# Issuing the stick-breaking scores of two heads interleaved on two halves of TensorE's rows, in one transformer stack on one Trainium2 core

## The chip, the core and the metric

One core of one Trainium2 chip runs the whole program as one launch. The metric is device time in microseconds (us): the median of several executions. The engines are TensorE (PE), VectorE (DVE), ScalarE (ACT), GpSimd (POOL) and SyncE (SP, which here issues the DMAs).

## What is computed

A block of one layer (dilated and sliding-window attention, gated, then an MLP) is followed by a block of two layers; width 1024, 512 positions, all in fp32. Each layer of the second block is a feed-forward part, a mixer with three branches, and a feed-forward part. The branches are stick-breaking attention (4 heads of 64), a chunkwise mLSTM (4 heads of 128) and MLA, a causal softmax attention (4 heads). The change touches the first of them. For one head, with z the scaled scores of a query against the keys before it:

```python
z = jnp.einsum('bhqd,bhkd->bhqk', qb, k[:, :, :n]) * scale      # scale = 64 ** -0.5
log_keep = jnp.where(mask, jax.nn.log_sigmoid(-z), 0.0)
later = ...                       # sum of log_keep over the keys between key and query
w = jnp.where(mask, jnp.exp(jax.nn.log_sigmoid(z) + later), 0.0)
out = jnp.einsum('bhqk,bhkd->bhqd', w, v[:, :, :n])
```

The kernel takes log_sigmoid from exp(-|z|) and a logarithm, so it needs |z|.

## The kernel before

**Main stream.** Nearly all of the time goes into products with weights. A weight tile is loaded by DMA (`load_w`, L346), rounded by ACT to `whi` (L348), its rest formed by DVE as `wlo` (L349); three products of 128x128 weights with up to 512 columns (`mm3`, `mm3t`) stand for one in fp32. In a layer's mixer the stream is: the latent projection (`c`), q, k and v of the stick-breaking branch, then `ml_proj`, which is eight feature tiles (PSUM tile `pf`, `fm_proj`) and two token projections (`pt`, `tm`) into `mlv` and `mgo`; then a wait for "mlw"; then per branch eight times a gate (`pgate`) and a branch product (`pbr`).

**Planner.** The order of PE is written out by hand, and no other engine's: `Loom` holds jobs (generators) beside the main stream. It has a clock of its own, `now`, which each matmul moves by a cost written in `mm` and `tr` (L175 and L182; 0.2135 for 512 columns of the weight products, twice 0.107 or 8.34e-4 a column for an fp32 product, 0.107 for a transpose). At the end of each half of a feature tile (12 products, 2.56 planner's us) and of each six products in a token projection (1.28), `turn()` runs, in the order of the list, every job whose due time has come and whose condition holds. A job that yields a number is due that much later; one that yields a function waits for it. Where the main stream itself must wait (`loom.wait`), jobs are stepped at once, whatever their due time, and their matmuls stand in PE's order with no weight product between. The jobs of a mixer are, in the order of the list, MLA (`mla_job`, then three workers that share 16 units of scores `mls`, transposes `mlT` and outputs `mlo`), stick-breaking (`sb_job`), and the gates of the mLSTM (`ml_gates_job`), which goes on only when "sb" and "ymla" are ready, makes `mwt` and sets "mlw".

**Slots.** The larger tiles live in a fixed set of places (`Slots`): 18 of 4352 bytes a partition and 5 of 2048. A tile takes the smallest place that fits. `room(...)` is the condition that so many places of these sizes are free. A place taken by the main stream without room steps jobs until there is some. In a mixer the large ones go to q, k, v of this branch (3), MLA's values and transposed heads (5, given back when its last unit is done), `ymla`, four `mlqk`, `ysb`, two `mlv`, two `mgo`, and the tiles of `stick_head`.

**The branch.** A pair of heads lies in the two halves of 128 partitions: head `hf` of pair `pr` has rows 64 hf to 64 hf + 63 of `q[:, pr]` and `k[:, pr]`. `stick_head` (L1365) runs once per head: it takes three score tiles at once, z, t and sp, each a place of 1024 columns (4096 bytes) and one of 256; writes the scores of four key blocks (512, 384, 256 and 128 query columns) into three banks `sbs` (L175) in three groups; ACT copies each bank to z (L1380) and its absolute value to t (L1381); Exp and Ln on t (L1383, L1384), two combinations on DVE into sp and z (L1385, L1386), and POOL masks the diagonals (L1395). After `T_SB` = 9.0 the running sums go out as four products `sbl`, from the last key block to the first; between two of them lies a DVE addition of one row (L1405) and a pause `T_SBR` = 1.5. Then DVE subtracts (L1408), ACT takes Exp (L1411), POOL masks (L1414), and t and sp are given back. When both heads of a pair have their weights, `sb_unit` waits `T_SBW` = 2.0 and issues the product with the values, `sbo`, whose two heads write the two column halves; z of both is given back. `sb_job` runs the four heads one after the other.

Of the kernel before, what the change touches and what calls it, by code (L numbers as in the profile page):

```python
# [12 lines left out]
AF = mybir.ActivationFunctionType  # L13
# [4 lines left out]
S = 512  # L18
# [108 lines left out]
class Net:  # L127
# [920 lines left out]
    def mixer(self, l, g_next):  # L1048
        nc, a, T, H, loom = self.nc, self.a, self.tiny, self.H, self.loom
        self.layer = l  # L1050
        w, b_in = a["w_in_2"][l], a["b_in_2"][l]
        V, A, G = nc.vector, nc.scalar, nc.gpsimd
# [28 lines left out]
        sbt = sq, sk, sv = [self.duo("sbq"), self.duo("sbk"), self.tok("sbv")]  # L1081
# [13 lines left out]

        W = {}

        def sb_unit(pr, hf):
            yield from self.stick_head(sq, sk, pr, hf, W)
            if len(W) < 2:  # L1100
                return
            yield T_SBW
            po = self.bank("sbo")
            for kb in range(TB):
                for hf in range(2):
                    h = 2 * pr + hf
                    self.mm(po[hf * 64:hf * 64 + 64, kb * 128:S], sv[:, kb, h * 64:h * 64 + 64], self.tri(W[hf], kb),
                            kb == 0, kb == TB - 1)
            H.put(*W[0], *W[1])
            W.clear()  # L1110
            if pr == 0:
                yield lambda: H.room(4096)
                ysb.append(self.duo("ysb"))
            A.copy(ysb[0][:, pr], po)
            if pr == 1:
                H.put(*sbt)
                ready.add("sb")

        def sb_job():
            for pr in range(2):  # L1120
                for hf in range(2):
                    yield from sb_unit(pr, hf)
        loom.add(sb_job())


# [236 lines left out]
        return t[1 if kb == 2 else 0][:, o:o + n]  # L1362


    def stick_head(self, q, k, pr, hf, W):  # L1365

        nc, H = self.nc, self.H
        V, A, G = nc.vector, nc.scalar, nc.gpsimd
        groups = ((1, 3), 0, 512, 1024), ((2,), 1, 0, 256), ((0,), 0, 0, 512)
        hs = slice(hf * 64, hf * 64 + 64)  # L1370
        yield lambda: H.room(4096, 4096, 4096, 1024, 1024, 1024)
        z, t, sp = self.tri_tiles("sbz"), self.tri_tiles("sbt"), self.tri_tiles("sbp")
        for kbs, i, c0, c1 in groups:
            ps = self.bank("sbs")
            c = 0
            for kb in kbs:
                n = S - kb * 128
                self.mm(ps[:, c:c + n], k[hs, pr, kb * 128:(kb + 1) * 128], q[hs, pr, kb * 128:S], True, True)
                c += n
            A.activation(z[i][:, c0:c1], ps[:, 0:c], AF.Copy, scale=0.125)  # L1380
            A.activation(t[i][:, c0:c1], ps[:, 0:c], AF.Abs, scale=0.125)  # L1381
        for i in range(2):
            A.activation(t[i], t[i], AF.Exp, scale=-1.0)  # L1383
            A.activation(t[i], t[i], AF.Ln, bias=1.0)  # L1384
            V.scalar_tensor_tensor(sp[i], z[i], 0.0, t[i], op0=ALU.max, op1=ALU.add)  # L1385
            V.scalar_tensor_tensor(z[i], z[i], 0.0, t[i], op0=ALU.min, op1=ALU.subtract)  # L1386

        keep = t[0][0:1, 0:768]
        own = {3: keep[:, 0:128], 2: keep[:, 128:384], 1: keep[:, 384:768]}
        for kb in (3, 2, 1, 0):  # L1390
            if kb:
                A.copy(own[kb], self.tri(sp, kb)[0:1])
                G.memset(own[kb][:, 0:1], 0.0)
            d = self.tri(sp, kb)[:, 0:128]
            G.tensor_mul(d, d, self.upper0)  # L1395
        yield T_SB
        pl = {1: self.bank("sbl"), 2: self.bank("sbl")}
        pl[3] = pl[1][:, 384:512]
        for kb in (3, 2, 1, 0):
            n = S - kb * 128  # L1400
            if kb == 0:
                pl[0] = self.bank("sbl")
            self.mm(pl[kb][:, 0:n], self.trigt, self.tri(sp, kb), True, True)
            if kb:
                V.tensor_add(self.tri(sp, kb - 1)[0:1, 128:n + 128], pl[kb][0:1, 0:n], own[kb])  # L1405
                yield T_SBR
        for i, c0, c1, kb in ((0, 512, 1024, 1), (1, 0, 256, 2), (0, 0, 512, 0)):
            V.tensor_sub(z[i][:, c0:c1], z[i][:, c0:c1], pl[kb][:, 0:c1 - c0])  # L1408
        H.put(*t, *sp)
        for i in range(2):  # L1410
            A.activation(z[i], z[i], AF.Exp)  # L1411
        for kb in range(TB):
            d = self.tri(z, kb)[:, 0:128]
            G.tensor_mul(d, d, self.upper)  # L1414
        W[hf] = z


    def ml_gates_job(self, ifg, W, ready):
# [225 lines left out]
```

## Time and profile before

| | us |
|---|---|
| median of three runs (lowest, highest) | 2348.06 (2347.34, 2348.90) |
| the profiled execution | 2348.01 |
| its span, first to last instruction | 2346.3 |
| PE busy | 2331.9 (99%) |
| DVE, ACT, POOL busy | 1275.5, 905.1, 381.3 |
| chain that ended last, share of PE | 98% |
| of it PE `sbs`, `sbl` | 1% each |

The page gives busy time by engine, then the span in slices, the DMA queues, the chain of work that ended last, and the costliest groups of instructions. A group's busy time is what its instructions cover, so that overlapping ones count once; the mean is of one instruction. An fp32 product shows as two records. All matmuls carry the line of the helper `mm` (L175) or `tr` (L182), so they are told apart by tile.

### The profile page before, as it was taken

The numbers are of one execution on the slowest core, as the hardware profiler recorded it, in microseconds if no ns is written. First come the engines' busy times: TensorE is split into PE (matmuls) and PEld (weight loads), VectorE is DVE, ScalarE is ACT, GpSimd is POOL, SyncE is SP. The second block draws the span as 40 slices with busy tenths as digits, with TensorE's granted clock in tenths as the row PEclk, the third lists the DMA queues.
The fourth block names the chain that finished last, engine by engine and source line by source line (L and its number), as shares of the span: only waits on it lengthen the run. The fifth ranks groups of instructions, "written<-read, shape, count | busy, mean of one in ns | idle before, by whom it ended". The sixth has DMA issues, their size and how long they took to land.

```text
span 2346.3 us, 28790 instructions
## 1 busy us (share of the span) xinstructions
PE 2331.9 (99%) x11064; PEld 1946.7 (83%) x11064; DVE 1275.5 (54%) x2214; ACT 905.1 (39%) x1510; POOL 381.3 (16%) x385
## 2 busy tenths in 40 slices
PE   8999999999999999999999999999999999999999
PEld 7899888888888888877888888888888778888887
DVE  7744556435355545785554554455458755446552
ACT  6645433222223223676333333223236572333321
POOL 2000014101022112211111321211211110113110
PEclk9999999999999999999999999999999999999999
DMA  4212432333323323322233333333232232323332
GB/s 137 64 55 73 121 96 90 101 97 95 103 86 100 101 92 98 87 65 85 72 90 99 99 95 94 94 95 99 90 101 82 72 86 58 105 81 108 91 102 87
DMA packets 250462, 213.71 MB, mean 91 GB/s; under 512 B 14166, under 2 KB 234068, under 8 KB 250324
## 3 DMA queue, kind: packets, MB, share of 16 engines
q1 hardware_dynamic: 250324, 211.87, 30.4%
q8 instruction: 87, 1.43, 0.2%
q14 instruction: 51, 0.42, 0.1%
HBM read 208.64 MB, written 3.19 MB: 90 GB/s over the span
## 4 chain that ended last, share of the span: by engine, by line
PE 98%; DMA 1%; ACT 0%; DVE 0%; SPq 0%; issue 0%; ACTq 0%
PE pd L175 15%; PE pgate L175 15%; PE pt L175 15%; PE pg L175 10%; PE pa L175 10%; PE pu L175 7%; PE pf L175 6%; PE po L175 5%; PE pbr L175 5%; PE mls L175 1%; PE sbs L175 1%; PE mnum L175 1%; PE sbl L175 1%; PE mss L175 1%; PE mlo L175 1%; PE s L175 1%
## 5 line engine op out<-in xcount | busy, mean ns | idle before, releaser
L349 DVE TENSOR_TENSOR wlo<-wraw,whi 128x1024 fp32r<-128x1024 f32 (+3 forms) x394 | 546.5, 1387 | 415.3 <-ACT whi L348 411.3
L348 ACT CAST whi<-wraw 128x1024 fp32r<-128x1024 f32 (+3 forms) x394 | 404.6, 1028 | 666.7 <-PE pg L175 141.9
L175 PE MATMUL pd<-hidh,whi 128*128 128x512 f32 x520 | 202.3, 389 | 0.0
L175 PE MATMUL pd<-hidl,whi 128*128 128x512 f32 x520 | 202.3, 389 | 0.0
L175 PE MATMUL pd<-hidh,wlo 128*128 128x512 f32 x520 | 202.3, 389 | 0.0
L175 PE MATMUL pgate<-xh,whi 128*128 128x512 f32 x512 | 201.2, 393 | 0.0
L175 PE MATMUL pgate<-xh,wlo 128*128 128x512 f32 x512 | 199.4, 390 | 0.0
L175 PE MATMUL pgate<-xl,whi 128*128 128x512 f32 x512 | 199.3, 389 | 0.0
L175 PE MATMUL pt<-whi,xh 128*128 128x512 f32 (+2 forms) x480 | 182.0, 379 | 0.0
L175 PE MATMUL pt<-whi,xl 128*128 128x512 f32 (+2 forms) x480 | 172.8, 360 | 0.0
L175 PE MATMUL pt<-wlo,xh 128*128 128x512 f32 (+2 forms) x480 | 172.5, 359 | 0.0
L175 PE MATMUL pa<-xl,whi 128*128 128x512 f32 x352 | 137.2, 390 | 0.7 <-DVE xl L438 0.7
L175 PE MATMUL pa<-xh,whi 128*128 128x512 f32 x352 | 137.6, 391 | 0.0
L175 PE MATMUL pg<-xh,whi 128*128 128x512 f32 x352 | 137.4, 390 | 0.0
L175 PE MATMUL pa<-xh,wlo 128*128 128x512 f32 x352 | 137.1, 389 | 0.0
L175 PE MATMUL pg<-xh,wlo 128*128 128x512 f32 x352 | 137.0, 389 | 0.0
L175 PE MATMUL pg<-xl,whi 128*128 128x512 f32 x352 | 137.0, 389 | 0.0
L549 POOL TENSOR_TENSOR t<-t,t 128x512 f32<-128x512 f32 x44 | 56.7, 1290 | 426.5 <-ACT whi L348 303.8
L175 PEld LDWEIGHTS pd<-hidh,wlo 128*128 128x128 f32 x520 | 97.6, 188 | 20.4
L175 PEld LDWEIGHTS pd<-hidl,whi 128*128 128x128 f32 x520 | 97.6, 188 | 20.3
L175 PEld LDWEIGHTS pd<-hidh,whi 128*128 128x128 f32 x520 | 97.6, 188 | 20.1
L175 PEld LDWEIGHTS pgate<-xh,wlo 128*128 128x128 f32 x512 | 96.1, 188 | 20.3
(488 smaller groups left out, 4671.2 us busy)
## 6 DMA issues: line engine op xcount, KB each, us to landing
wraw<-in_w_in_dram SPq DMA_DIRECT2D x116, 512.0 KB, 3.6
wraw<-in_ffn_wi_dram SPq DMA_DIRECT2D x176, 256.0 KB, 3.0
wraw<-in_ffn_wo_dram SPq DMA_DIRECT2D x34, 512.0 KB, 3.5
wraw<-in_w_up_dram SPq DMA_DIRECT2D x32, 512.0 KB, 3.8
wraw<-in_w_out_dram SPq DMA_DIRECT2D x24, 512.0 KB, 3.4
wraw<-in_w_down_dram SPq DMA_DIRECT2D x24, 512.0 KB, 3.9
wraw<-in_w_in_dram SPq DMA_DIRECT2D x32, 256.0 KB, 2.9
wraw<-in_ffn_wo_dram SPq DMA_DIRECT2D x12, 384.0 KB, 3.1
```

The source lines that it names most:

```text
L175: self.nc.tensor.matmul(out, lhsT, rhs, start=start, stop=stop)
L348: nc.scalar.copy(hi, raw)
L349: nc.vector.tensor_sub(lo, raw, hi.bitcast(F32))
L549: nc.gpsimd.tensor_mul(t2, t2, t1)
```

## The change

The scores move out of `stick_head` into a new `stick_scores`, which runs once per pair. It takes the z tiles of both heads, and for each of the three groups a bank per head; the matmuls of the two heads alternate, one on partitions 0 to 63, the next on 64 to 127. ACT copies both banks to z, and the job pauses by 1.0 after each group. `stick_head` then takes t and sp alone, and the absolute value is taken from z in SBUF, once per tile, not from PSUM once per group.

```diff
-        def sb_unit(pr, hf):
-            yield from self.stick_head(sq, sk, pr, hf, W)
+        def sb_unit(pr, hf, z):
+            yield from self.stick_head(z)
+            W[hf] = z
...
             for pr in range(2):
+                z = []
+                yield from self.stick_scores(sq, sk, pr, z)
                 for hf in range(2):
-                    yield from sb_unit(pr, hf)
+                    yield from sb_unit(pr, hf, z[hf])
...
-    def stick_head(self, q, k, pr, hf, W):
+    def stick_scores(self, q, k, pr, z):
 
         nc, H = self.nc, self.H
-        V, A, G = nc.vector, nc.scalar, nc.gpsimd
-        groups = ((1, 3), 0, 512, 1024), ((2,), 1, 0, 256), ((0,), 0, 0, 512)
-        hs = slice(hf * 64, hf * 64 + 64)
-        yield lambda: H.room(4096, 4096, 4096, 1024, 1024, 1024)
-        z, t, sp = self.tri_tiles("sbz"), self.tri_tiles("sbt"), self.tri_tiles("sbp")
-        for kbs, i, c0, c1 in groups:
-            ps = self.bank("sbs")
+        yield lambda: H.room(4096, 4096, 1024, 1024)
+        z += [self.tri_tiles("sbz") for _ in range(2)]
+        for kbs, i, c0, c1 in ((1, 3), 0, 512, 1024), ((2,), 1, 0, 256), ((0,), 0, 0, 512):
+            ps = [self.bank("sbs") for _ in range(2)]
             c = 0
             for kb in kbs:
                 n = S - kb * 128
-                self.mm(ps[:, c:c + n], k[hs, pr, kb * 128:(kb + 1) * 128], q[hs, pr, kb * 128:S], True, True)
+                for hf in range(2):
+                    hs = slice(hf * 64, hf * 64 + 64)
+                    self.mm(ps[hf][:, c:c + n], k[hs, pr, kb * 128:(kb + 1) * 128], q[hs, pr, kb * 128:S], True, True)
                 c += n
-            A.activation(z[i][:, c0:c1], ps[:, 0:c], AF.Copy, scale=0.125)
-            A.activation(t[i][:, c0:c1], ps[:, 0:c], AF.Abs, scale=0.125)
+            for hf in range(2):
+                nc.scalar.activation(z[hf][i][:, c0:c1], ps[hf][:, 0:c], AF.Copy, scale=0.125)
+            yield 1.0
+
+    def stick_head(self, z):
+
+        nc, H = self.nc, self.H
+        V, A, G = nc.vector, nc.scalar, nc.gpsimd
+        yield lambda: H.room(4096, 4096, 1024, 1024)
+        t, sp = self.tri_tiles("sbt"), self.tri_tiles("sbp")
         for i in range(2):
+            A.activation(t[i], z[i], AF.Abs)
             A.activation(t[i], t[i], AF.Exp, scale=-1.0)
...
-        W[hf] = z
```

## Rows read from the trace of the kernel before

**Rows 1.** The page's first part: busy us (share of the span) and instructions by engine.
```profile
PE 2331.9 (99%) x11064; PEld 1946.7 (83%) x11064; DVE 1275.5 (54%) x2214; ACT 905.1 (39%) x1510; POOL 381.3 (16%) x385
```
**Rows 2.** PE's waits: who for whom, us in total, times, longest.
```profile
PE colT L182 <- DMA rows<-in_ln_g_dram: 4.7, 1, 4.7
PE xtp L182 <- DMA xin<-in_x_dram: 4.0, 1, 4.0
```
**Rows 3.** PE's groups by shape: line, tile, count | busy us, mean ns | idle.
```profile
L175 PE MATMUL sbs<-sbq,sbk 64*128 64x256 f32 x16 | 4.8, 377 | 0.0
...
L175 PE MATMUL s<-kbT,qb0T 64*128 64x256 f32 x24 | 3.4, 397 | 0.0
```
**Rows 4.** PE in order of time, first score insertion: start us, us, records merged.
```profile
983.06 0.60 PE L182 MATMUL mT<-ident,mq 128*96 128x128 f32 x4
983.59 2.42 PE L175 MATMUL sbs<-sbq,sbk 64*128 64x384 f32 x8
985.94 0.64 PE L182 MATMUL mT<-ident,mq 128*96 128x128 f32 x4
```
**Rows 5.** Chain of waits that ended last, 975 to 1130 us: start us, us, what.
```profile
1033.87 2.31 PE sbo L175 x16
1036.17 2.35 PE sbs L175 x8
...
1085.01 6.84 PE pt L175 x30
1092.07 2.74 PE pt L175 x12
...
1101.41 0.86 PE sbl L175 x2
...
1107.48 12.46 PE pt L175 x54
1119.94 5.44 PE pgate L175 x24
```
**Rows 6.** ACT in order of time, 1080 to 1086 us, fourth head.
```profile
1080.62 0.60 ACT L1380 ACTIVATE sbz<-sbs 128x512 f32<-128x512 f32 x1 [0.91 <-PE sbs L175]
...
1083.08 1.41 ACT L1383 ACTIVATE sbt<-sbt 128x256 f32<-128x256 f32 x2
...
1085.84 0.46 ACT L1495 ACTIVATE mwt<-mwt,bcol 128x128 f32<-128x128 f32 x1
```
**Rows 7.** Tile sbs, ACT's readers: ns least/median/most, first and last start.
```profile
L1381 ACT ACTIVATE sbt<-sbs x24: 402/591/644, 985.3 to 1883.3; 128x512 f32<-128x512 f32 x16, 128x256 f32<-128x256 f32 x8
```
**Rows 8.** PE in order of time, 1076 to 1082 us, where MLA ends.
```profile
1078.47 1.00 PE L175 MATMUL mlo<-mv,mpT 128*128 128x64 f32 x8
1079.40 2.42 PE L175 MATMUL sbs<-sbq,sbk 64*128 64x384 f32 x8
```
**Rows 9.** DVE in order of time, 1091 to 1103 us, fourth head's rows.
```profile
1092.98 0.27 DVE L1405 TENSOR_TENSOR sbp<-sbl,sbt 1x128 f32<-1x128 f32 x1
...
1095.71 0.40 DVE L1405 TENSOR_TENSOR sbp<-sbl,sbt 1x256 f32<-1x256 f32 x1
...
1098.69 0.54 DVE L1405 TENSOR_TENSOR sbp<-sbl,sbt 1x384 f32<-1x384 f32 x1 [2.24 <-PE sbl L175]
```
**Rows 10.** POOL in order of time, 1087 to 1106 us.
```profile
1087.14 1.51 POOL L1395 TENSOR_TENSOR sbp<-sbp,upper 128x128 f32<-128x128 f32 x1 [26.57 <-DVE sbp L1385]
...
1104.34 1.54 POOL L1414 TENSOR_TENSOR sbz<-sbz,upper 128x128 f32<-128x128 f32 x3 [6.91 <-ACT sbz L1411]
```
**Rows 11.** ACT in order of time, 1103 to 1112 us.
```profile
1103.15 1.05 ACT L1411 ACTIVATE sbz<-sbz 128x1024 f32<-128x1024 f32 x1
...
1110.19 1.03 ACT L526 CAST yph<-ysb 128x1024 fp32r<-128x1024 f32 x1
```
**Rows 12.** Two stretches at the start: busy us (count) by engine, granted clock, DMA.
```profile
10.00:15.00 5.00, 4.12 (x20) 4.13 (x21) 4.36 (x6) 2.63 (x5) 0.00 (x0) 1.00 0.58 158
15.00:20.00 5.00, 5.00 (x44) 5.00 (x44) 2.59 (x4) 3.24 (x6) 0.00 (x0) 1.00 0.46 131
```

## The prediction

> **What bounds the kernel now.** I read the page first: TensorE (PE) is busy for 2331.9 of 2346.3 us [rows 1]. The view of who waited for whom agrees: its longest waits are 4.7 and 4.0 us, both at the start for the first loads [rows 2]. So the end moves by what PE issues, and by any new hole in its stream. ScalarE (ACT) and VectorE (DVE) have slack: work saved there is worth nothing, and their durations matter only where PE has nothing else to do. I then looked at the touched matmuls (by shape, then in order of time) and at the end of the mixer's branch phase, where the planner's order decides whether such holes open.
>
> **Part 1, the scores on PE.** Of an fp32 matmul the trace has two records. One head's eight score records take 2.35 us in the chain of waits [rows 5]. A full-height fp32 product of 512 columns takes 0.86 us in the chain [rows 5], so 1280 columns stream in 2.5 x 0.86 = 2.15; the remaining 0.20 is the uncovered first weight load and the step out of the half-height form. Two more pieces lie around it [rows 4]: the last of the four transposes ahead has streamed by 983.50 (from 983.06, 0.11 apart, since 128 columns are a quarter of 0.43), and the scores start at 983.59 (0.09); the four transposes behind take 0.64 and not 0.60 (0.04). One insertion therefore costs 0.33 us beyond its columns, one head 2.48, and eight heads (2 layers, 2 pairs, 2 heads) 19.8 us.
>
> After: do two halves really run side by side in fp32? The change's own form is not in the trace, but two neighbours are. The 16 records of sbo, two heads on the two column halves with the same 1280 columns each, take 2.31 us where the scores of one head take 2.35 [rows 5]. The first block's scores use the two row halves: 24 records of 256 columns with a mean of 397 ns cover 3.4 us, where 16 of the same shape from one half cover 4.8 [rows 3], so 0.14 us each against 0.30. I take full overlap: 2.15 us of columns a pair. But the pair now comes as three separate pieces with a pause of 1.0 between, so three insertions where there were two: 2.15 + 3 x 0.33 = 3.14 a pair, four pairs 12.6. **Gain: 19.8 - 12.6 = 7.2 us.** Bounds: with no overlap the columns take 4.30 a pair, 5.29 in all, which is a loss of 1.3 us; if the three pieces coalesced it would be a gain of 9.9.
>
> The Trainium skill, "TensorE: Matmul & The Clock Gate", Part 3, measured only 3.07x for four row tiles. By that ratio two halves would give about 1.54x (an estimate from that page), the columns of a pair would take 2.79, and the gain would be 4.7. The rows above show no such loss, so I keep 7.2.
>
> **Part 2, absolute value from SBUF.** A head loses three ACT operations from PSUM (0.40 to 0.64 us, median 0.59) [rows 7] and gains two on 1024 and 256 columns; Exp on the same two tiles takes 1.41 for both [rows 6], so ACT's time changes by about -0.2 us a head. A bank is also read once instead of twice. All of it lies under PE's main stream; worth nothing by itself.
>
> **Part 3, slots and order: where the price is.** PE's order is written by Loom, and a step goes out when its due time and its slots allow. Following the code's own costs, in planner's us from the first score matmul of a layer: before, head 1 begins at 0, its first sbl is due at 11.1, and pair 0's sbo goes out at 46.9. In the change the pair's three pieces go out at three turns (0, 5.1, 9.0), head 1 begins at 13.5, its sbl run from 22.6 to 34, head 2's from 44 to 56, and sbo at 58.6.
>
> Then the large slots. Before, pair 1 found five free at 51.2 and its first head took z, t and sp at once; the second head needs three more and stood until MLA gave back five. The trace shows it: the eight scores of the fourth head start at 1079.40, right behind MLA's last mlo at 1078.47, 43 us after those of the third at 1036.17 [rows 5, 8]. In the change pair 1's scores start at 62.9 and take two large slots for both z; two are left, and the main stream takes them for mlv at 65.5, before the third piece is out. Count then: q, k, v 3, MLA 5, ymla 1, mlqk 4, ysb 1, mlv 2, z 2 = 18 of 18. **Both** heads of pair 1 now stand until MLA ends, where before only one did. By the same costs MLA ends at 99.9 (92.8 before). The third head's sbl then run from 108.8 to 118.9, the fourth head's are due at 127.9, and the main stream, out of its last projection, waits for mlw from 125.3. So the fourth head's four sbl and sbo come with nothing between them. Before, 54 projection records (12.46 us) still stood behind sbo [rows 5].
>
> The price in a layer, from rows: each sbl must wait for its predecessor's row. A record's result comes 0.16 us after its stream (a 256-column record lasts 0.377 [rows 3] and streams a quarter of 0.86). The addition takes 0.27, 0.40, 0.54 [rows 9]. DVE began the first 0.91 after its sbl had ended at 1092.07 [rows 5, 9], and the third at once, having sat idle until then [rows 9]; I take the middle, 0.47. Links: 0.90 + 1.03 + 1.17 = 3.1. Behind the last sbl come the subtraction, Exp (1.05) and the first of three masks (1.54 for three from 1104.34; I give the first half of it): in the trace from 1102.27, where that sbl ended, to 1105.1 [rows 5, 10, 11]; with the 0.16 that is 3.0, less 0.43 of sbo's first head that needs none of it: 2.5. **Sum 5.6 a layer, 11.2 for both.** Bounds: DVE free at once and the masks hidden, 3.8 a layer. Above: the fourth head's first sbl late. Its cover is 30 projection records, 6.84 us [rows 5], against 8.0 from the first copy to the end of the first mask before (1080.62 to 1088.65) [rows 6, 10]; ACT, though, worked on mwt at 1085.84 [rows 6], 19 us ahead of the sbo behind which its step goes out, so I take it as ready early: 0 to 2.5. The branch product behind the first gate needs ysb split: 3.7 us from sbo's end (1107.48) to that of the cast (1111.2), and a subtraction behind it, against 5.44 of gate [rows 5, 11]: 0 to 2.5.
>
> A last upper term is the clock. At the start, after idling, 20 records took 4.12 us of PE, in the next 5 us there were 44 of much the same size, 0.21 against 0.11 us each, though the column of the granted clock shows full for both [rows 12]; about 4 us at half pace lose 2.1. If the thin stretch lowers it, that is 2.1 more a layer. The Trainium skill, "TensorE: Matmul & The Clock Gate", Part 1, says that an idle engine is throttled; no row shows it for holes of a microsecond, so the sum leaves it out.
>
> **The sum.** The profiled execution took 2348.0 us (its span is 2346.3, 1.7 lie around it), the same as the median of 2348.06. 2348.0 - 7.2 + 11.2 = **2352.0 us**.
>
> **Rivals.**
> - *The chain stays covered* (faster). If MLA ends some 10 planner's us sooner than I work out, or the third head finds its slots ahead of mlv, the fourth head's sbl fall between projection records as at 1091 to 1105 now, and the 7.2 stand alone: 2340.8. For it: the planner runs on its own costs, a turn's threshold can tip by 0.1. Against: 18 slots are counted, not timed.
> - *Exposed further* (slower). If pair 0's sbo slips past the mlv request, pair 1's scores stand as well until MLA ends; then the 9.0 between a head's begin and its sbl is open on PE too. Per layer 5.6 + 9 = 14.6, so 2348.0 - 7.2 + 29.2 = 2370. It decides from a slip of about two turns (6 us).
> - *The halves don't overlap* (the change doesn't do what it says): 2348.0 + 1.3 + 11.2 = 2360.5. Against it stand [rows 3].
> - *Clock lowered* in the thin stretch: 2352.0 + 4.2 = 2356.2; counted inside my own case's range.
>
> **How the numbers follow.** What a measurement of this kernel can tell from no change is about 0.2%, 4.7 us. My case 0.63 (own range 2347 to 2360: 3.8 to about 10 us a layer), of which 0.33 within 0.2%, 0.29 slower, 0.01 faster; chain covered 0.20; exposed further 0.12; no overlap 0.05. Faster 0.21, same 0.33, slower 0.46. The point lies just inside no change, while the tail is on the slow side. The range 2340 to 2364 leaves out the longer exposure and the edges.
>
> **What would show it.** Right: 16 score records in three pieces a pair, sbs of one shape covering about half of the sum of its means; sbs of pair 1 with a long gap to its first sbl; at the end of the mlo projection sbl, sbl, sbl, sbl, sbo with PE idle by about 5 us a layer, released by DVE, and pgate directly behind sbo. Wrong: sbo still followed by projection records (then faster), or scores at 2.4 us a head.

## The result, and the profile of the changed kernel

| | before | after |
|---|---|---|
| median (lowest, highest), us | 2348.07 (2347.34, 2348.90) | 2362.36 (2360.25, 2365.91) |
| the profiled execution, us | 2348.01 | 2361.38 |
| its span, us | 2346.3 | 2359.6 |
| mean granted clock of TensorE | 1.000 | 0.998 |

The ratio is 1.0063, 95% interval [1.0047, 1.0079]: slower by more than this kernel's measurement is uncertain. The time lies 10.4 us above the predicted point, at the upper end of the stated range (2340 to 2364), and above the 2347 to 2360 that the prediction gave its own case.

The page of after still shows PE as the bound (compare [rows 1]):

```profile
PE 2335.2 (99%) x11064; PEld 1941.3 (82%) x11064; DVE 1276.3 (54%) x2214; ACT 908.7 (39%) x1502; POOL 374.4 (16%) x385
```

PE is busy 3.3 us longer in a span that is 13.3 longer, so 10 us are new holes. The busy time is no measure of the work saved: `sbs` covers 7.5 us less than before (11.9 for 19.4), but `sbo` 5.7 more (15.5 for 9.8), since its first product now runs alone ahead of the wait, and in layer 2 at a lowered clock. PE's waits of after (who for whom, us in total, times, longest) name them; before, nothing above 0.7 us stood there but the loads at the start [rows 2]:

```profile
PE sbl L175 <- DVE sbp L1416: 5.3, 6, 1.2
PE colT L182 <- DMA rows<-in_ln_g_dram: 4.6, 1, 4.6
PE mlT L182 <- ACT mp L1322: 3.2, 6, 1.2
PE xtp L182 <- DMA xin<-in_x_dram: 3.0, 1, 3.0
PE sbo L175 <- POOL sbz L1425: 2.7, 4, 1.5
```

**The scores.** PE in order of time, the first pair's three pieces in after (start us, us, records merged):

```profile
982.23 1.14 PE L175 MATMUL sbs<-sbq,sbk 64*128 64x384 f32 x8
983.30 0.64 PE L182 MATMUL mT<-ident,mq 128*96 128x128 f32 x4
...
987.07 0.70 PE L175 MATMUL sbs<-sbq,sbk 64*128 64x256 f32 x4
987.70 0.64 PE L182 MATMUL mT<-ident,mq 128*96 128x128 f32 x4
...
991.02 1.13 PE L175 MATMUL sbs<-sbq,sbk 64*128 64x512 f32 x4
992.08 0.28 PE L182 MATMUL rowif<-ident,gi 128*16 128x128 f32 x1
```

From the start of a piece to that of the next matmul it is 1.07, 0.63 and 1.06 us, 2.76 a pair. Before, one head took 983.59 to 985.94, 2.35 [rows 4], so 4.70 a pair. The gain is 1.94 a pair, 7.8 us for four.

**The end of the branch phase.** PE in order of time, layer 1 of after; in square brackets the idle time ahead and its releaser:

```profile
1113.64 0.40 PE L175 MATMUL pt<-whi,xl 128*128 128x512 f32 x1
1113.88 0.39 PE L175 MATMUL sbl<-sbp,trigt 128*128 128x128 f32 x2
1115.49 0.67 PE L175 MATMUL sbl<-sbp,trigt 128*128 128x256 f32 x2 [1.23 <-DVE sbp L1416]
1116.96 0.88 PE L175 MATMUL sbl<-sbp,trigt 128*128 128x384 f32 x2 [0.80 <-DVE sbp L1416]
1118.48 1.12 PE L175 MATMUL sbl<-sbp,trigt 128*128 128x512 f32 x2 [0.64 <-DVE sbp L1416]
1119.54 1.07 PE L175 MATMUL sbo<-sbz,sbv 128*64 128x512 f32 x2
1122.15 2.37 PE L175 MATMUL sbo<-sbz,sbv 128*64 128x512 f32 x14 [1.54 <-POOL sbz L1425]
1124.44 0.50 PE L175 MATMUL pgate<-xh,whi 128*128 128x512 f32 x1
```

Four sbl and sbo with no projection between them, then the gates: the exposed chain of the prediction. What a group of inserted matmuls costs is read as the distance from the last main-stream product ahead of it to the second one behind it (the first is still disturbed), less the usual 0.23 for each of the two steps. Before, the same records cost 0.24, 0.45, 0.66 and 0.87 for the four sbl and 2.66 for sbo, 4.9 us; now they cost 10.7. So 5.8 us are exposed in layer 1.

**The middle of the phase.** The chain of waits of after, 1030 to 1052 us, shows two holes that the prediction doesn't have:

```profile
1032.59 0.45 PE sbl L175 x2
...
1033.06 0.41 DVE sbp L1416
1033.47 0.07 DVE mnm L1321
...
1033.56 0.61 ACT mp L1322 x2
...
1034.22 0.44 PE mlT L182 x2
...
1042.31 1.05 ACT whi L348
...
1043.39 1.22 DVE wlo L349
1044.61 0.61 DVE sbz L1419
...
1045.24 1.06 ACT sbz L1422
...
1046.38 0.47 POOL sbz L1425
...
1046.89 2.37 PE sbo L175 x12
```

In the first, MLA's transpose needs an exponential of ACT, that needs the maximum `mnm` of DVE, and `mnm` stands in DVE's queue behind the stick-breaking addition, which itself waits for an sbl that PE has just finished: a hole of 1.20 us. In the second, pair 0's sbo needs subtraction, Exp and mask; the subtraction stands behind the split of a weight tile (`whi`, then `wlo`). From the first record of sbo to the next other matmul it is 3.72 us in after and 2.30 before. Both come in each layer. Before, the last sbl ahead of pair 0's sbo (1033.80) started 4.27 us earlier; in after it starts at 1042.34, 3.13 ahead of sbo:

```profile
1029.53 1.02 PE L175 MATMUL sbl<-sbp,trigt 128*128 128x512 f32 x2
```

A third hole stands ahead of these two, in each layer again. PE in order of time, behind the first head's last sbl, which starts at 1016.54:

```profile
1017.74 0.72 PE L182 MATMUL mlT<-ident,mp 128*128 128x128 f32 x2 [0.17 <-ACT mp L1322]
1018.67 0.33 PE L182 MATMUL mlT<-ident,mp 128*128 128x128 f32 x1 [0.21 <-ACT mp L1322]
```

The transposes wait for exponentials of ACT, and the last of these for a maximum `mnm` that stands in DVE's queue behind a stick-breaking subtraction (L1419, 1017.36 to 1018.03). Counted as above, this sbl and the three transposes cost 2.31 us (1016.31 to 1019.08); before, such an sbl cost 0.87 and three such transposes 0.34. So 1.1 us are lost in a layer.

**The clock.** Two stretches of layer 2's chain in after (length, then busy us and count of PE, PEld, DVE, ACT, POOL; granted clock; DMA share, GB/s):

```profile
1921.00:1925.00 4.00, 1.97 (x8) 0.85 (x6) 3.37 (x7) 1.46 (x2) 0.10 (x1) 1.00 0.55 136
1925.00:1932.00 7.00, 5.86 (x12) 1.80 (x13) 3.04 (x9) 5.26 (x15) 1.63 (x4) 0.51 0.24 74
```

PE covered 1.97 of 4 us, and then ran for 7 us at a granted clock of 0.51, the lower of its two levels (1.2 for 2.4 GHz); with the gates behind, it was back at 1.00. In layer 1 the same order of matmuls ran at 1.00 throughout (1110 to 1130 us). From the first of the eight sbl records to the 41st of the gates it took 21.34 us there and 23.05 here: 1.7 us.

### The profile page after: what moved, and what is told of

The parts are those of the page before. It is cut to its first block, busy times and chain, and to the rows that moved or that the text cites. A ratio compares the mean times of both kernels' runs of the same rounds, so it can differ in the third digit from the quotient of the medians.

```text
span 2359.6 us, 28775 instructions
## 1 busy us (share of the span) xinstructions
PE 2335.2 (99%) x11064; PEld 1941.3 (82%) x11064; DVE 1276.3 (54%) x2214; ACT 908.7 (39%) x1502; POOL 374.4 (16%) x385
## 4 chain that ended last, share of the span: by engine, by line
PE 94%; DVE 2%; ACT 2%; issue 1%; DMA 1%; POOL 0%; SPq 0%; ACTq 0%; POOLq 0%
PE pd L175 15%; PE pgate L175 15%; PE pt L175 14%; PE pg L175 10%; PE pa L175 10%; PE pu L175 7%; PE po L175 5%; PE pbr L175 5%; PE pf L175 4%; DVE wlo L349 1%; PE mnum L175 1%; PE mss L175 1%; PE s L175 1%; PE mlo L175 1%; PE mls L175 1%
```

## The experiments

Theory A is that of the prediction: the scores gain what was worked out, and the order that the slots force gives it back at the end of the phase. Its rivals are B, that the row-half form itself costs (no full overlap), and C, that the pauses do, since they make three insertions of two. Each kernel was compared with runs of the kernel before on the same chip (medians 2347.69 to 2348.31).

**Slots.** The two small z tiles of a pair share one small place, as do t and sp of a head, so that none of them takes a large one; and `mlv` is taken when it is first written.

```diff
-        yield lambda: H.room(4096, 4096, 1024, 1024)
-        z += [self.tri_tiles("sbz") for _ in range(2)]
+        yield lambda: H.room(4096, 4096, 2048)
+        u = H.get("sbz2", [128, 2, 256])
+        z += [(H.get("sbz", [128, 1024]), u[:, i], u) for i in range(2)]
...
-        vml += [H.get("mlv", [128, 2, 544]) for _ in range(2)]
...
+            if b % 2 == 0:
+                vml.append(H.get("mlv", [128, 2, 544]))
```

> The changed kernel with only its slots mended: the two 256-column tiles that go together share one small place, and the two mlv tiles are taken when the first result is there to be written, not 21 us ahead. Scores, halves, pauses and due times stay as in the change. By the planner's costs the third head then gets its places before MLA ends, and sbo of pair 1 goes out some 10 us ahead of the end of the last projection. Theory A (the loss is the chain of the fourth head that has nothing beside it): PE's waits on the additions and masks at the end of the phase are gone, and what is left is the gain on the scores, 7.2 us, less the few waits in the middle of the phase: 2341 to 2347. Rival B (the row-half form costs PE time around it, or does not overlap): stays at 2355 to 2364. Rival C (the three pieces with pauses cost it): stays near 2360.

Measured: 2345.41 us, ratio 0.9988 [0.9979, 0.9997]: 17 us faster than the change with the same scores, and faster than the kernel before. Its waits of PE:

```profile
PE xtp L182 <- DMA xin<-in_x_dram: 5.1, 1, 5.1
...
PE mlT L182 <- ACT mp L1322: 1.4, 4, 0.4
```

No wait of sbl or sbo is left, and the granted clock is 1.000. Projection products stand on both sides of the last sbo (the first line merges 16 records):

```profile
1096.18 3.13 PE L175 MATMUL sbo<-sbz,sbv 128*64 128x512 f32 x16
1099.24 0.50 PE L175 MATMUL pt<-whi,xh 128*128 128x512 f32 x1
```

So the places decide. But A put the loss at the end of the phase alone, and that this run doesn't show: the same edit also took away the 1.20 us ahead of mlT, and pair 0's sbo takes 2.30 again. What came back is the loss of both parts of the phase.

**The late order alone.** The kernel before, with its old scores, but pair 1 made to begin when MLA has ended:

```diff
             for pr in range(2):
+                if pr:
+                    yield lambda: "mla" in ready
+                    yield 5.0
                 for hf in range(2):
```

> The kernel before, with its scores one head at a time and the absolute value from PSUM, where pair 1 alone is put off until MLA has ended and 5.0 planner's us more: its fourth head's products fall at the planner's times of the changed kernel (first sbl due 2.6 behind the end of the projection). Nothing of the change is in it. Theory A: slower by the exposed chain alone, 6.5 us in each layer and one or two for a lowered clock, so 2360 to 2365, with PE waiting for the additions and the masks. Rivals B and C: nothing of what they blame is there, so 2346 to 2351.

Measured: 2368.95 us, ratio 1.0088 [1.0074, 1.0102], above what A expected. The order by itself loses 20.6 us, more than in the change, and the trace shows two reasons: here the fourth head's first sbl is late as well, by 1.9 us a layer (an upper term of the prediction, 0 to 2.5 there), and the clock fell in both layers (the wait, then a stretch of layer 1 with columns as above, clock 0.74; in layer 2, from 1915 to 1935 us, it was 0.89). The middle of the phase loses nothing here: no wait of mlT stands in the list, and pair 0's sbo takes 2.30.

```profile
PE sbl L175 <- POOL sbp L1398: 3.9, 2, 1.9
```

```profile
1110.00:1130.00 20.00, 15.41 (x48) 7.66 (x47) 13.03 (x26) 15.03 (x37) 4.10 (x11) 0.74 0.19 54
```

**No pauses.** The change without `yield 1.0` behind each group:

```diff
-            yield 1.0
```

> The changed kernel without the pause of 1.0 after each group, so that a pair's 16 score records come in one piece. The planner's order at the end of the phase is the same as in the changed kernel: both heads of pair 1 stand until MLA ends, the fourth head's products fall behind the projection. Theory A: only two insertions a pair are saved, 0.33 us each, 2.6 us in all: 2356 to 2362. Rival C: back at 2340 to 2347. Rival B: about 2360.

Measured: 2357.25 us, ratio 1.0038 [1.0025, 1.0052]. The pauses cost 5.1 of the 14.3 us; the chain at the end is still there (PE waits 5.1 us for sbl on DVE, 2.0 for sbo on POOL) and so is the lowered clock in layer 2 (0.83 in 1915 to 1935 us). The time lies in A's range, with 5.1 us where A has 2.6; C explains a part, not the loss.

**All three together**, and the planner charged for the scores with half their columns (`self.loom.now -= c * 16.68e-4` in each group):

> The mended slots of the first run, no pauses, and the planner charged for a pair's scores with one head's columns, since the halves run side by side. Sbo of pair 1 goes out about 20 planner's us ahead of the end of the last projection. Theory A: the whole gain of one piece a pair, 9.9 us, less waits in the middle of the phase: 2337 to 2343. Rival B: at or above 2350.

Measured: 2344.92 us, ratio 0.9986 [0.9977, 0.9994], two above the expectation. Here the scores gained the most, and MLA took it back. The scores of a whole pair in order of time, and PE's longest wait:

```profile
982.56 2.43 PE L175 MATMUL sbs<-sbq,sbk 64*128 64x384 f32 x16
984.92 0.64 PE L182 MATMUL mT<-ident,mq 128*96 128x128 f32 x4
```

```profile
PE mlT L182 <- ACT mp L1322: 5.7, 6, 1.4
```

The 16 records of two heads take 2.36 us (982.56 to 984.92). The eight of one head took 2.35 before [rows 4]. The halves overlap fully: B falls.

**The same, charged in full**, to see whether the charge of half caused MLA's waits (packed tiles, late `mlv`, no pauses):

> The kernel of the run with all mended, but the planner charges the scores of both heads in full again: small tiles of two heads (and of t and sp) share one place of 2048 bytes, mlv is taken later, no pauses between the three groups. If the MLA waits of 5.7 us in that run came from the charge of half (which brings MLA's steps closer together than TensorE's time allows), they go back to about the 1.4 of the run with the pauses, and the time is that run's 2345.4 less two insertions a pair (4 x 2 x 0.33 = 2.6): 2342 to 2344. If they come from the three groups standing in one piece (ScalarE then copies six banks in a row, and MLA's exponentials behind them are late), they stay, and the time is 2344.5 to 2347.

Measured: 2345.18 us, ratio 0.9990 [0.9981, 0.9998], with the same 5.7 us of MLA's waits. PE's order is the same, matmul for matmul, in both kernels, so the charge moved nothing. The second reading holds in this: the waits come with the groups in one piece. Two in each layer are large, 1.40 us at 1016.88 and 1.15 at 1051.42 in layer 1; the chain of waits ahead of the later one runs through ACT's copies of pair 1's banks (1044 to 1047 us) and its Abs, Exp and Ln, much as that reading has it. Ahead of the earlier one it runs through stick-breaking work in DVE's queue (1013 to 1015 us), which that reading does not have.

**Pauses in pair 0 alone**, in the kernel of the run on slots:

```diff
-            yield 1.0
+            if pr == 0:
+                yield 1.0
```

> The kernel with packed small tiles and mlv taken later, with the pauses between the three groups kept in pair 0 alone. Pair 1's three pieces become one: two insertions less in each layer, 4 x 0.33 = 1.3 us: 2345.4 - 1.3 = 2344.1, 2343 to 2345, if the MLA waits that came when all pauses were taken away (5.7 us for 1.4) belong to pair 0's groups, which stand ahead of MLA's first units. If they belong to pair 1's, 2345 to 2348.

Measured: 2350.40 us, ratio 1.0010 [1.0001, 1.0019]. Neither reading gave this time. Of the 1.40 us at 1016.88 in the last run, 0.4 are left, so they came with pair 0's groups in one piece. But pair 1 in one piece (2.35 us for 16 records) starts its heads earlier, into the middle of MLA's units, and the waits that appear are those of MLA and sbl for each other's work on DVE, 3.1 us beside the 1.5 on ACT:

```profile
PE mls L175 <- DVE mpT L1331: 1.6, 2, 0.8
PE sbl L175 <- DVE mlm L1318: 1.5, 2, 0.7
```

One turn of the planner, moved, was worth 5 us against 1.3 of insertions saved.

**Order of issue.** The change, with the first head's matmuls of a group ahead of the second head's:

```diff
-                for hf in range(2):
-                    hs = slice(hf * 64, hf * 64 + 64)
-                    self.mm(ps[hf][:, c:c + n], ...)
+            for hf in range(2):
+                c = 0
+                hs = slice(hf * 64, hf * 64 + 64)
+                for kb in kbs:
+                    n = S - kb * 128
+                    self.mm(ps[hf][:, c:c + n], ...)
```

> The change, with one edit: within a group the matmuls of the first head are issued first, then those of the second head, in place of one by one in turn. Rival 1: a record may start as soon as the one issued before it has started and its own rows are free, but not ahead of it. Then the second head starts with the last record of the first: in columns, 1920 for 1024 in the first group, 768 for 512 in the second, 1536 for 1024 in the third, so 4224 for 2560, at 0.86 us for 1024: 3.55 us a pair for 2.15, 1.4 more for each of four pairs, 5.6 in all, 2368 us, and the 16 score records of the first piece start at uneven distances. Rival 2: the two halves draw on the queue independently of the order (the first block's scores come as two of one half, then two of the other, and covered half of the sum of their durations): 2361 to 2363, as the change.

Measured: 2363.63 us, ratio 1.0065 [1.0052, 1.0079], the same as the change. The first group, columns as in the first PE view:

```profile
982.38 1.14 PE L175 MATMUL sbs<-sbq,sbk 64*128 64x384 f32 x8
983.45 0.64 PE L182 MATMUL mT<-ident,mq 128*96 128x128 f32 x4
```

It takes 1.07 us as in the change; 1920 columns in a row, as rival 1 has it, would be 1.6. Rival 2 holds. What the change gains comes from having both heads' matmuls next to each other, not from alternating them.

**The absolute value alone.** The kernel before, with one edit:

```diff
-            A.activation(t[i][:, c0:c1], ps[:, 0:c], AF.Abs, scale=0.125)
         for i in range(2):
+            A.activation(t[i], z[i], AF.Abs)
             A.activation(t[i], t[i], AF.Exp, scale=-1.0)
```

> The kernel before, with one edit: the absolute value is taken from z in SBUF, once for each of its two tiles, and not from the score banks. My prediction priced this part at nothing, since ScalarE has slack (busy 39%) and TensorE's order is the same: 2347 to 2349 us. The rival says that ScalarE's order is part of the 10 us by which the change came out above my point (the two operations stand between the copies and Exp, and MLA's exponentials queue on the same engine): then 2350 us or more.

Measured: 2352.77 us, ratio 1.0022 [1.0013, 1.0031]. The part that I had priced at nothing costs 5.1 us with the same order of matmuls. Four views of this run, one after the other: the longer of PE's two new waits (the other is sbl for the POOL step L1393, 0.9 us); the row copies on ACT and the masks on POOL ahead of the second head's first sbl, in order of time; and that sbl on PE:

```profile
PE sbl L175 <- POOL sbp L1395: 2.0, 2, 1.0
```

```profile
1018.92 1.06 ACT L348 CAST whi<-wraw 128x1024 fp32r<-128x1024 f32 x1
1019.87 1.01 ACT L1392 COPY sbt<-sbp 1x128 f32<-1x128 f32 x3
```

```profile
1018.27 1.51 POOL L1395 TENSOR_TENSOR sbp<-sbp,upper 128x128 f32<-128x128 f32 x1 [4.23 <-DVE sbp L1385]
1020.22 0.09 POOL L1393 MEMSET sbt<- 1x1 f32 x1 [0.44 <-ACT sbt L1392]
1020.27 1.50 POOL L1395 TENSOR_TENSOR sbp<-sbp,upper 128x128 f32<-128x128 f32 x1
```

```profile
1021.83 0.49 PE L175 MATMUL sbl<-sbp,trigt 128*128 128x128 f32 x2 [1.00 <-POOL sbp L1395]
```

Before, the row copies ran ahead of the cast on ACT, and this sbl went out at 1020.97 without a wait:

```profile
1019.27 1.02 ACT L1392 COPY sbt<-sbp 1x128 f32<-1x128 f32 x3
1020.19 1.05 ACT L348 CAST whi<-wraw 128x1024 fp32r<-128x1024 f32 x1
```

Now the cast comes first on ACT, POOL waits for the copies, and PE for POOL. These waits are 2.9 of the 4.1 us by which the profiled execution is longer.

**The absolute value by groups**, right behind each copy, from z in SBUF:

```diff
-            A.activation(t[i][:, c0:c1], ps[:, 0:c], AF.Abs, scale=0.125)
+            A.activation(t[i][:, c0:c1], z[i][:, c0:c1], AF.Abs)
```

> The kernel before, with the absolute value taken from z in SBUF, but group by group right behind each copy, as three pieces of 512, 256 and 512 columns, where the run of the absolute value alone took it once for each whole tile. That run lost 5.1 us, with the same order of matmuls. Theory O: it lost them through order, because the whole-tile operation can't start before the last group is copied and Exp and Ln of the large tile then end 0.8 us later, and because other work of ScalarE slips in between; by pieces that is mended: 2347 to 2350. Theory S: it is the source itself (each operation must wait for the copy's end before it can read z, and the row copies and masks behind are late whatever the pieces): 2351 to 2354.

Measured: 2354.27 us, ratio 1.0027 [1.0018, 1.0037]. Theory O falls: the pieces mend nothing. Other waits stand in the list (mlT 2.3 us on ACT, carryT 1.3 on DVE), and pair 0's sbo takes 2.96 for 2.30. The number lies just above S's range; whether it is the dependence on z or only the other order that follows from it on ACT is open, since no run held that order fixed.

**Pair 0's sbo later.** The change, with one number altered:

```diff
-            yield T_SBW
+            yield T_SBW if pr else 5.0
```

> The change, with one number altered: pair 0's sbo is due 5.0 after the last step of its second head, not 2.0, so that one more half feature tile stands between the two. Theory M (part of the 10 us by which the change came out above my point are waits in the middle of the branch phase): sbo of pair 0 covers 3.72 us in the change and 2.30 before, since its masks are late; with more cover the 1.4 us a layer go, and the end of the phase stays as it is: 2362.4 - 2.8 = 2359.6, 2358 to 2361. My rival of the prediction (exposed further): sbo now goes out behind the request for mlv, pair 1's scores find no places until MLA ends, and the time is about 2368 to 2372. If the wait only moves elsewhere, 2361 to 2364.

Measured: 2361.66 us, ratio 1.0061 [1.0047, 1.0074]. Pair 0's sbo is mended as M says: 2.30 us for 3.72 in both layers. But the time stays, as the last reading has it, since the end took most of it back: the last chain of layer 1 costs 12.8 us in place of 10.7, that of layer 2 0.5 less than in the change. Two lines of PE in layer 1 in order of time; the granted clock from 1110 to 1130 us is 0.83:

```profile
1114.65 0.49 PE L175 MATMUL sbl<-sbp,trigt 128*128 128x128 f32 x2 [0.54 <-POOL sbp L1406]
...
1119.09 2.08 PE L175 MATMUL sbl<-sbp,trigt 128*128 128x512 f32 x2 [0.64 <-DVE sbp L1416]
```

The first sbl is now late, and the fourth runs 2.08 us for 1.12, at the lowered clock, in layer 1 too. My rival of 2368 to 2372 falls: pair 1's scores start at 1052.3 us, some 36 us ahead of MLA's last mlo (1088.7), although sbo now goes out behind the request for `mlv`.

## Why the prediction came out as it did

**The scores: right.** Full overlap was taken, with three insertions a pair: 2.15 of columns and 0.20 for each piece between starts, 2.75; measured 2.76. The gain was 7.8 where 7.2 was worked out. The Trainium skill, "TensorE: Matmul & The Clock Gate", Part 3, measured 3.07x for four row tiles; scaled to two, as in the prediction, that is 2.79 for the columns alone (an estimate). This trace does not agree with the scaling: 2.36 us for the whole pair in one piece, edges included.

**The slots: right.** Both heads of pair 1 stood until MLA ended (scores from 1049.19 on, MLA's last mlo at 1085.91, the third head's first sbl at 1096.62, where it was 1048.04 before), and the fourth head's sbl and sbo came behind the last projection with nothing between. The run on slots shows that the places are the cause.

**The price of the exposed chain: right in sum.** 5.6 a layer were worked out, 5.8 measured in layer 1. The parts agree less well: without the 0.16 of each result, the holes between the sbl are 1.23, 0.80 and 0.64 where 0.74, 0.87 and 1.01 had been worked out, since DVE was busy with `mgo` and `wlo` at the first two and idle only at the third.

**The sum: 9.4 us short in the profiled execution** (2361.4 for 2352.0). The direction and the largest term, the exposed chain, were right. That the time still fell inside 2340 to 2364 is luck: the room up there was meant for a lowered clock, a late sbl and a late branch product at the end of the phase, and it was mostly filled by holes in the middle of the phase that the working did not have. The terms that it lacked:

- *The middle of the phase, the largest.* Holes of 1.20 us ahead of mlT, 1.42 us more of sbo and 1.1 at the earlier mlT, in each of two layers, 7.4 us. The step that failed is the walk of the planner. It had the last sbl at 56 and pair 0's sbo at 58.6, and I priced the chain from last sbl to sbo (3.0) only at the end of the phase. 2.6 of cover is less than 3.0, so the numbers stood there. Counted as the 3.0 is, from where the last sbl has streamed (0.86 after its start), the cover was 3.41 us before (1030.39 to 1033.80) and 2.27 after (1043.20 to 1045.47). The chain took 3.69 there, to 1046.89. So about half of the 1.42 stood in the prediction's own numbers (3.0 less 2.27), and the other half is the subtraction's place behind the weight split in DVE's queue. That MLA's transposes would wait behind stick-breaking work in DVE's queue stood nowhere in my working: I had looked at PE's order and at sums of the other engines, not at who stands behind whom in their queues.
- *The clock.* Named, priced at 2.1 a layer, and left out of the sum since no row showed it for short holes. It cost 1.7, in layer 2 alone.
- *The absolute value.* "Worth nothing by itself" is wrong: alone it costs 5.1 us. How much of that sits in the change can't be told. The waits that it makes in its own run (sbl on POOL) are not in the list of after, and a run with the other parts and the old source wasn't made, since t has no places at that time.
- *The rest.* -0.6 (scores) + 0.4 (chains) + 7.4 + 1.7 - 1.1 (the first loads, which landed sooner) is 7.8. The other 1.6 I did not assign.

**The rivals.** The chain covered was worked out at 2340.8. Made real by the places, it gave 2345.4: it brings back the 14.3 us lost and 2.7 more, but not the whole gain on the scores. Part of what is missing is in its trace: 1.4 us of MLA's waits, its last sbo at 3.06 us in each layer where it was 2.46 before, and a first load that came 1.1 us later (5.1 for 4.0). "Exposed further" had a wrong threshold: pair 0's own two z places are given back with its sbo, so pair 1's z could follow even behind the request for `mlv`, as in the run with the later sbo. No overlap is refuted. The lowered clock is real, in one layer of two.

**A version that beats both** came out of the tests: packed small tiles and a late `mlv`, 2345.4, and without pauses 2344.9 to 2345.2. That is 0.1% below the kernel before, with intervals that end just short of 1.

## What to carry to other kernels

Where one engine is busy 99% of the time under an order written by hand, other engines' slack in sum is no cover: an edit there is priced by the queue position of what the next hand-placed matmul needs. When a step is moved, walk every hand-over behind it and hold its chain against the new distance, in the middle as well as at the end. And two tiles that are held earlier than before can cost more than the matmuls that they make cheaper: count the places first, and try the order alone without the gain, and the gain with the places mended.

## What the runs showed of the hardware

- Two row halves of TensorE, fp32, 64 rows each: 16 records of two heads take 2.36 us, eight of one head 2.35. They overlap whether the program alternates them or puts one head's behind the other's (1.07 us for the group either way).
- The granted clock fell to half for some 7 us (0.51 from 1925 to 1932 us) where PE was not idle for long at a time. The holes ahead of it were 0.6 to 1.2 us each; PE was busy for 1.97 of the 4 us before. Which layer it hit differed between kernels with the same kind of chain. The Trainium skill, "TensorE: Matmul & The Clock Gate", Part 1, describes such a fall by short idle times between groups of matmuls; the trace agrees in kind, with the 0.51 above.
- POOL's mask of 128x128 took 1.51 us alone and 1.50 right behind, in the run of the absolute value, where three in a row took 1.54 in [rows 10]. No run here says what sets its time.
